# Hybrid decoder layer, one core: the last two blocks of the output projection multiplied together, and the up stage's tiles laid on the memory that comes free

## The chip, the cores and the metric

One core of a Trainium2 chip runs the whole layer in one program. The metric is the device time of one execution in microseconds (us), the median of several runs. Profiles are of one execution; times in rows count from the start of its span.

## What is computed

A decoder layer on x of 2048 tokens by 1024, all in float32. The first half mixes tokens with two groups of heads (attention and an mLSTM), whose outputs stand side by side in 1024 columns. The seam that matters here is what follows:

```python
mixed = jnp.concatenate([o_diff, o_mlstm], axis=-1) @ w_out   # 1024 x 1024
x = x + rmsnorm(mixed, norm_mix_post)
h = rmsnorm(x, norm_mlp_pre)
u = jnp.square(jax.nn.relu(h @ w_up))                         # 1024 x 4096
x = x + rmsnorm(u @ w_down, norm_mlp_post)
```

## The kernel before

**Matmuls.** TensorE multiplies float32r. Each operand is kept as a high part (a cast) and a low part (the rest), and each product is three matmuls of 128x128 by 128x512 (`mm3`, lines 91 to 95, and `product`, line 964).

**Output projection** (`out_proj`, line 838). The 2048 tokens are 16 blocks of 128, taken in the order `seq`; the first eight belong to g = 0, the last eight to g = 1. For each block, `gather` (line 853) loads the head outputs `od` into a `raw` tile, transposes them in two halves on TensorE into a PSUM tile `tp` of the two-buffer pool `psT`, and writes the operand into a tile `p`, of which there are two (pools `shp` and `ot`). `project` (line 858) runs over the eight weight rows `w[kc]` (128 rows of w_out each, 8 KB a partition, all in the pool `wo`) and both halves of the columns into two PSUM banks `po`: 48 matmuls. `residual` (line 869) loads the block's x into `xt` (one buffer), squares `po` on ACT, scales by an rsqrt on VectorE (DVE), adds x on POOL into `x1` (one buffer), stores x1, and makes the normed `t` for the MLP.

**Operands of the up stage.** The up and the down product use seven sub-products in place of eight, so the up stage wants seven combinations B1 to B7 of the normed tokens for each g. `spread` (line 908) transposes `t` of a block in two halves into `tp`, forms the combinations with DVE and POOL, and `parts` (line 895) casts each one on ACT and subtracts on DVE. For g = 0, B1, B2, B6 and B7 (`NEAR`) go straight into the tiles `ops` on the right side of the memory. All others go through a tile `hl` (two buffers) and a store into `Bd` in DRAM, 512 KB in runs of 512 B. A block of even place in a pair stores two parts for g = 1, one of odd place five (the last two through POOL). The spread of block n - 2 and the gather of block n + 1 stand between the weight rows of block n.

**Up stage** (`MlpUp`, line 973; `UpPair`, line 1020). For g = 0 and 1 there are 8 batches of two pairs; each batch takes the steps 1, 2, 6, 7, 5, 3, 4 (`UP_ORDER`), and a step is 12 matmuls for each pair. Its left operand comes from a row of w_up (`wr`, 256 KB), combined on DVE, cast on ACT (line 1059) and subtracted on DVE (line 1026) into a tile `w`. Steps 1, 6, 5 and 3 add into a bank A, copied by ACT between steps (`snap`); steps 2 and 7 begin a bank B, step 4 adds to the second. Tiles of one name are taken in turn from a ring of places (`Rotation`, line 820). B5, B3 and B4 of g = 0 are loaded (`load_op`, 2 MB each) into the pool `far`.

**What sets the order.** The framework lists the instructions of each engine and of SP's queue in the order in which its own timing model finds them ready, the program's order breaking ties; on the chip each engine works its list strictly in order. All loads and stores here are issued from SP's queue. A tile that lies on the memory of a closed pool waits for the readers of the tiles that it covers.

**The seam.** In `body` the pools `raw`, `wo` and `shp` lie at the left, `ops` at the right. Step 1 of the first two pairs (`first`, line 985) has two `wr` tiles, two `w` tiles and two PSUM banks of its own at the right (`wre`, `wqe`, `psE`). All else of the up stage is opened in `run` (line 994), behind the projection's pools: at the left first `far` and `sp`, then 15 tiles `u`, 12 `wr` and 4 `w`.

Of the kernel before, what the change touches and what calls it, by code (L numbers as in the profile page):

```python
# [20 lines left out]
S = 2048  # L21
# [77 lines left out]
def body(ctx: ExitStack, tc: tile.TileContext, a: dict, out: bass.AP, phases="ABCD"):  # L99
# [39 lines left out]
    with ExitStack() as mid:  # L139
        mix = phase_mix(tc, a, sc, ident, late)  # L140
        next(mix)
        for _ in first:
            pass
        raw = mid.enter_context(tc.tile_pool(name="raw", bufs=2, reuse_waits="tile"))
        wo = mid.enter_context(tc.tile_pool(name="wo", bufs=1, reuse_waits="tile"))
        w_out = [wo.tile([128, 2, D], F32R, name=f"wo{kc}") for kc in range(KC)]
        shp = mid.enter_context(tc.tile_pool(name="shp", bufs=1, reuse_waits="tile"))
        late.update(raw=raw, w_out=w_out, shp=shp)
        for _ in mix:
            pass  # L150
# [5 lines left out]
        early.append(hp.enter_context(  # L156
            tc.tile_pool(name="psE", bufs=1, side="right", reuse_waits="tile", space=PSUM)))
        up = out_proj(tc, a, sc, ident, ops, w_out, dn, raw, shp, late["oT"],
                      lambda: MlpUp(tc, a, sc, ops, hpool, *early))
    up.run()  # L160
    hp.close()
    mlp_down(tc, a, sc, out)
# [657 lines left out]
class Rotation:  # L820


    def __init__(self, shape, dt, name, *pools):
        self.shape, self.dt, self.name, self.places, self.n = shape, dt, name, [], 0
        for p, n in pools:
            self.extend(p, n)
# [8 lines left out]
        return pool.tile(self.shape, self.dt, name=name, bufs=1)  # L835


def out_proj(tc, a, sc, ident, ops, w, dn, raw, shp, oT, start_up):
    nc = tc.nc
    with ExitStack() as ctx:  # L840
        def pool(name, bufs, **kw):
            return ctx.enter_context(tc.tile_pool(name=name, bufs=bufs, reuse_waits="tile", **kw))

        ld = pool("ld", 2)
        ot = pool("ot", 1)
        cc = pool("cc", 1)
        t1 = pool("t1", 2)
        x1p = pool("x1p", 1)
        so = pool("so", 2)
        psO = pool("psO", 4, space=PSUM)  # L850
        psT = pool("psT2", 2, space=PSUM)
# [6 lines left out]
        def project(oT, between=()):  # L858
            po = [psO.tile([128, 512], F32, name="po") for _ in range(2)]
            for kc in range(KC):  # L860
                for hf in range(2):
                    sl = slice(hf * 512, hf * 512 + 512)
                    mm3(nc, po[hf], [oT[:, 0, kc, :], oT[:, 1, kc, :]], [w[kc][:, 0, sl], w[kc][:, 1, sl]],
                        kc == 0, kc == KC - 1)
                if kc % 2 == 0 and kc // 2 < len(between):
                    between[kc // 2]()
            return po

        def residual(tt, po):
            rows = slice(tt * 128, (tt + 1) * 128)  # L870
            xt = ld.tile([128, D], F32, name="xt", bufs=1)
# [68 lines left out]
        g2 = cc.tile([128, D], F32, name="g2")  # L940
        nc.sync.dma_start(g2, a["g_mlp_pre"].partition_broadcast(128))
        seq = [g * 8 + c + o * 4 for g in range(2) for c in range(4) for o in range(2)]
        h2 = {}
        for n, tt in enumerate(seq):
            between = []
            if n >= 2:
                half = spread(seq[n - 2], h2.pop(n - 2))
                between += [partial(half, 0), partial(half, 1)]
            cur = oT
            if n + 1 < NT:  # L950
                oT, half = gather(seq[n + 1], n + 1)
                between += [partial(half, 0), partial(half, 1)]
            po = project(cur, between)
            h2[n] = residual(tt, po)
        up = start_up()
        for n in (NT - 2, NT - 1):
            up.first(n - NT + 2)
            half = spread(seq[n], h2.pop(n))
            half(0)
            half(1)  # L960
        return up


def product(nc, ps, lhs, rhs, n, first, last):
# [8 lines left out]
class MlpUp:  # L973

    def __init__(self, tc, a, sc, ops, hpool, wre, wqe, psE):
        self.tc, self.nc, self.a, self.sc, self.ops, self.hpool = tc, tc.nc, a, sc, ops, hpool
        self.pools = wre, wqe, psE
        self.wr = Rotation([128, 512], F32, "wr", (wre, 2))  # L980
        self.wq = Rotation([128, 2, 512], F32R, "w", (wqe, 2))
        self.psA = Rotation([128, 512], F32, "A", (psE, 2))
        self.batch = [UpPair(self, 0, m) for m in range(2)]

    def first(self, m):

        self.batch[m].matmuls(1)

    def load_op(self, g, i):
        t = (self.hpool if i in NEAR else self.far).tile([128, 2, 4, 512], F32R, name=f"B{i}")  # L990
        self.nc.sync.dma_start(t.bitcast(F32), self.sc["Bd"][g, i])
        return t

    def run(self):
        wre, wqe, psE = self.pools
        with ExitStack() as ctx:
            def pool(name, bufs, **kw):
                return ctx.enter_context(self.tc.tile_pool(name=name, bufs=bufs, reuse_waits="tile", **kw))

            self.far = pool("far", 1)  # L1000
            self.sp = Rotation([128, 512], F32, "s", (pool("sp", 1), 5))
            self.up = Rotation([128, 512], F32, "u", (pool("up", 1), 15))
            self.wr.extend(pool("wr", 1), 12)
            self.wq.extend(pool("wq", 1), 4)
            self.psA.extend(pool("psA", 1, space=PSUM), 2)
            self.psB = Rotation([128, 512], F32, "B", (pool("psB", 1, space=PSUM), 4))
            for i in (5, 3, 4):
                self.ops[i] = self.load_op(0, i)
            for g in range(2):
                if g == 1:  # L1010
                    for i in UP_ORDER:
                        self.ops[i] = self.load_op(1, i)
                for n in range(8):
                    pairs = self.batch if (g, n) == (0, 0) else [UpPair(self, g, 2 * n + m) for m in range(2)]
                    for i in UP_ORDER:
                        for p in pairs:
                            p.run(i)


class UpPair:  # L1020
    def __init__(self, up, g, j):
        self.up, self.nc, self.g, self.j = up, up.nc, g, j
        self.begun = False

    def tt(self, out, x, y, op):
        self.nc.vector.tensor_tensor(out, x, y, op=op)  # L1026
# [24 lines left out]
        return {7: self.a21, 5: self.s1, 4: self.a22}[i]  # L1051

    def matmuls(self, i):
        if i == 1 and self.begun:
            return
        self.begun = True
        src = self.left(i)
        w = self.up.wq()
        self.nc.scalar.copy(w[:, 0], src)  # L1059
# [273 lines left out]
```

## Time and profile before

| | us |
|---|---|
| median of 3 runs | 2559.36 (2558.26 to 2561.15) |
| the profiled execution's own time | 2563.28 |
| its span, first to last instruction | 2561.4 |
| TensorE busy with matmuls | 2425.0 |
| DVE, ACT, POOL busy | 1456.0, 1065.2, 440.1 |

The span is cut into 40 slices of 64 us in the page's strips. PE stands for TensorE's matmuls; PEclk is the clock that it was granted, in tenths of full speed. In chains and timelines each line has its start in us, its length in us, and what ran; in square brackets stands the idle time before it and what ended that.

### The profile page before, as it was taken

To read this page: it belongs to the slowest core of one execution; us is meant where nothing else is said; L and a number is where in the kernel's file an instruction comes from. 1 tells how busy PE (TensorE), PEld (TensorE's weight loads), DVE (VectorE), ACT (ScalarE), POOL (GpSimd) and SP (SyncE) were. 2 spreads that over 40 slices of the span, in tenths; PEclk is the share of its full clock that TensorE was granted. 3 is DMA by queue.
4 is the path that set the end of the run, shared out by engine and by line. 5 is a ranking of instruction groups with operands and counts; after the bars stand their busy time and mean duration, and the time that the engine had idled before them with its cause. 6 is when DMAs were issued, how large, how long until landed. Compare 5 with 4: busy or idle time off the path is not lost.

```text
span 2561.4 us, 34625 instructions
## 1 busy us (share of the span) xinstructions
PE 2425.0 (95%) x12030; PEld 2040.0 (80%) x12030; DVE 1456.0 (57%) x3132; ACT 1065.2 (42%) x2103; POOL 440.1 (17%) x724
## 2 busy tenths in 40 slices
PE   8999999989879799999939999999999999999998
PEld 6888889987668687888828888888888888887886
DVE  4483441016657588576647667666665543333885
ACT  7210112326656577644524344444444332332433
POOL 0002222104635354432300000000000000000423
PEclk9999999998889899999969999999999999999999
DMA  9323432257653634255774345844358664444784
GB/s 320 130 78 91 125 109 85 55 133 167 145 115 75 148 88 113 83 177 181 236 266 164 136 157 174 350 161 168 133 176 305 222 221 169 146 143 167 282 288 144
DMA packets 296751, 424.35 MB, mean 166 GB/s; under 512 B 23584, under 2 KB 170416, under 8 KB 295040
## 3 DMA queue, kind: packets, MB, share of 16 engines
q1 hardware_dynamic: 296224, 421.94, 51.5%
q8 instruction: 95, 1.56, 0.3%
q14 instruction: 80, 0.66, 0.1%
q0 software_dynamic: 352, 0.20, 0.1%
HBM read 283.56 MB, written 138.49 MB: 165 GB/s over the span
## 4 chain that ended last, share of the span: by engine, by line
PE 76%; DMA 11%; DVE 6%; POOL 2%; ACT 2%; issue 2%; SPq 0%; POOLq 0%; DVEq 0%; ACTq 0%
PE pd L969 16%; PE A L969 14%; PE B L969 10%; PE pp L93 7%; PE pp L94 7%; PE pp L95 7%; DMA br<-in_w_down_dram 3%; PE pv L656 3%; PE s L573 3%; PE po L93 2%; DMA E<-Md 2%; PE po L94 2%; PE po L95 2%; PE tp L651 2%; DMA wb<-Wd 1%
## 5 line engine op out<-in xcount | busy, mean ns | idle before, releaser
L969 PE MATMUL pd<-bo,ao 128*128 128x512 f32 x2688 | 613.8, 390 | 8.3 <-DVE y L1153 4.8
L969 PEld LDWEIGHTS pd<-bo,ao 128*128 128x128 f32 x2688 | 506.2, 188 | 115.8 <-issue 5.2
L969 PE MATMUL A<-B,w 128*128 128x512 f32 x1536 | 359.3, 389 | 0.0
L969 PEld LDWEIGHTS A<-B,w 128*128 128x128 f32 x1536 | 288.3, 188 | 59.7
L969 PE MATMUL B<-B,w 128*128 128x512 f32 x1152 | 274.4, 392 | 19.2 <-ACT w L1059 19.2
L93 PE MATMUL pp<-w,xT 128*128 128x512 f32 (+1 forms) x768 | 271.3, 358 | 9.3 <-ACT w L230 7.8
L94 PE MATMUL pp<-w,xT 128*128 128x512 f32 (+1 forms) x768 | 273.2, 356 | 0.0
L95 PE MATMUL pp<-w,xT 128*128 128x512 f32 (+1 forms) x768 | 271.1, 355 | 0.0
L969 PEld LDWEIGHTS B<-B,w 128*128 128x128 f32 x1152 | 217.9, 189 | 65.0 <-ACT w L1059 19.7
L1211 POOL TENSOR_TENSOR y<-y,g 128x512 f32<-128x512 f32 x32 | 49.2, 1560 | 1183.6 <-ACT jk L1205 1120.2
L1178 ACT CAST ao<-ar 128x1024 fp32r<-128x1024 f32 x112 | 117.8, 1052 | 287.5 <-PE pd L969 150.5
L1153 DVE TENSOR_TENSOR ao<-ar,ao 128x1024 fp32r<-128x1024 f32 x112 | 139.3, 1243 | 152.3 <-ACT ao L1178 152.2
L1026 DVE TENSOR_TENSOR w<-wr,w 128x512 fp32r<-128x512 f32 x224 | 154.0, 689 | 105.0 <-ACT w L1059 103.9
L573 PE MATMUL s<-K,Q 128*128 128x512 f32 (+3 forms) x640 | 193.9, 418 | 13.6 <-DVE p L577 6.6
L1059 ACT CAST w<-wr 128x512 fp32r<-128x512 f32 x224 | 138.8, 621 | 130.6 <-PE B L969 116.8
L656 PE MATMUL pv<-V,pT 128*128 128x128 f32 x1088 | 158.2, 290 | 31.5 <-ACT pT L653 22.9
L656 PEld LDWEIGHTS pv<-V,pT 128*128 128x128 f32 x1088 | 147.4, 202 | 44.0 <-ACT pT L653 26.2
L586 ACT ACTIVATE p<-p,nm 128x128 f32<-128x128 f32 (+15 forms) x128 | 153.5, 1200 | 33.2 <-DVE nm L585 22.1
L93 PEld LDWEIGHTS pp<-w,xT 128*128 128x128 f32 x768 | 144.4, 188 | 25.9 <-ACT w L230 8.7
L577 DVE TENSOR_SCALAR_CACHE_REDUCE p<-s 128x512 f32<-128x512 f32 x192 | 129.0, 684 | 51.6 <-PE s L573 28.4
L94 PEld LDWEIGHTS pp<-w,xT 128*128 128x128 f32 x768 | 144.5, 188 | 15.2 <-DVE w L231 0.3
L95 PEld LDWEIGHTS pp<-w,xT 128*128 128x128 f32 x768 | 144.3, 188 | 15.1
(249 smaller groups left out, 3566.0 us busy)
## 6 DMA issues: line engine op xcount, KB each, us to landing
ud<-u SPq DMA_DIRECT2D x224, 256.0 KB, 2.8
ar<-ud SPq DMA_DIRECT2D x112, 512.0 KB, 4.1
br<-in_w_down_dram SPq DMA_DIRECT2D x224, 256.0 KB, 4.0
wr<-in_w_up_dram SPq DMA_DIRECT2D x128, 256.0 KB, 3.6
Bd<-hl SPq DMA_DIRECT2D x40, 512.0 KB, 3.9
B<-Bd SPq DMA_DIRECT2D x10, 2048.0 KB, 13.8
Q<-Qd SPq DMA_DIRECT2D x128, 128.0 KB, 4.7
raw<-in_xT_dram SPq DMA_DIRECT2D x32, 256.0 KB, 5.0
```

The source lines that it names most:

```text
L93: nc.tensor.matmul(ps, lhs[0], rhs[0], start=first, stop=False)
L94: nc.tensor.matmul(ps, lhs[0], rhs[1], start=False, stop=False)
L95: nc.tensor.matmul(ps, lhs[1], rhs[0], start=False, stop=last)
L573: nc.tensor.matmul(ps[:, :w], Q[:, var, c, qo:qo + 128], Ks[h, j][:, c, 0:w], start=(var == 0), stop=(var == 1))
L577: nc.vector.tensor_scalar(dst, ps[:, :w], 0.0, None, op0=ALU.add, op1=ALU.max, accum_out=mx[:, c, j:j + 1])
L586: nc.scalar.activation(pc[:, :W], pc[:, :W], AF.Exp, bias=nm[:, c:c + 1], accum_out=Z[:, c:c + 1])
L656: nc.tensor.matmul(pv, pT[:, i * 128:(i + 1) * 128], Vs[h, j][:, i, :], start=(b == 0), stop=(b == nb - 1))
L969: nc.tensor.matmul(ps, l[i], r[j], start=(first and k == 0 and m == 0), stop=(last and k == n - 1 and m == 2), skip_group_check=True)
L1026: self.nc.vector.tensor_tensor(out, x, y, op=op)
L1059: self.nc.scalar.copy(w[:, 0], src)
L1153: nc.vector.tensor_tensor(out, x, y, op=op)
L1178: nc.scalar.copy(l[:, 0], u)
```

## The change

The last two blocks are no longer multiplied one after the other. Block 13 carries the gathers of both 14 and 15; `project` then takes a list of operands and goes through the weight rows once, so that each row is used for both blocks before the next. For this there are three tiles `p` (a new pool `otp`) and three pairs of banks for `po`, one of which is `psE`. The projection's other pools move to the right side. When the joint loop is written, the left pools are closed (`mid.close()`), and the up stage's tiles are opened at the left on the rows of `raw`, `wo`, `shp` and `otp` in this order: 10 `wr`, 4 `w`, 5 `s`, `far`, 3 `u`. Its banks B and A follow on those of `po`, and at the end 12 `u`, 4 `wr`, 1 `w` and two banks B at the right on the projection's pools and on `psT`. So there are 14 `wr` as before, 5 `w` in place of 6, 15 `u`. Steps 1, 2 and 6 of the first batch and the loads of B5 and B3 are written between the residuals and the spreads of blocks 14 and 15; the load of B4 behind them. `first` and `begun` go.

```diff
-        early = [hp.enter_context(tc.tile_pool(name=n, bufs=1, side="right", reuse_waits="tile"))
-                 for n in ("wre", "wqe")]
...
+        up = MlpUp(tc, a, sc, ops, hpool, psE)
+        out_proj(tc, a, sc, ident, ops, w_out, dn, raw, shp, late["oT"], mid, up)
     up.run()
...
-            oT = (shp if n % 2 == 0 else ot).tile([128, S], F32, name="p")
+            oT = otp.tile([128, S], F32, name=f"p{n % 3}") if n % 3 else shp.tile([128, S], F32, name="p")
...
+        def project(n, oTs, between):
+
+            po = [[(psE if (n + i) % 3 == 1 else psO).tile(
+                [128, 512], F32, name=f"A{hf}" if (n + i) % 3 == 1 else f"po{(n + i) % 3}{hf}", bufs=1)
+                for hf in range(2)] for i in range(len(oTs))]
             for kc in range(KC):
...
+                for i, oT in enumerate(oTs):
+                    for hf in range(2):
+                        sl = slice(hf * 512, hf * 512 + 512)
+                        mm3(nc, po[i][hf], [oT[:, 0, kc, :], oT[:, 1, kc, :]], [w[kc][:, 0, sl], w[kc][:, 1, sl]],
+                            kc == 0, kc == KC - 1)
+                for half in between.pop(kc, ()):
+                    half()
             return po
...
+        nxt = [oT]
+        for n in range(NT - 2):
+            cur = nxt
+            nxt = []
+            between = {}
             if n >= 2:
...
+                between[0], between[2] = ([f] for f in halves(n - 2))
+            for i, m in enumerate([n + 1] if n < NT - 3 else [NT - 2, NT - 1]):
+                t, half = gather(seq[m], m)
+                nxt.append(t)
+                between[4 + 2 * i] = [partial(half, 0)] if n < NT - 3 else [partial(half, 0), partial(half, 1)]
+                if n < NT - 3:
+                    between[6] = [partial(half, 1)]
+            h2[n] = residual(seq[n], project(n, cur, between)[0])
+        last = NT - 2, NT - 1
+        between = {}
+        for n in last:
+            a0, a1 = halves(n - 2)
+            between[4 * (n - NT + 2)], between[4 * (n - NT + 2) + 2] = [a0], [a1]
+        po = project(NT - 2, nxt, between)
+        mid.close()
+        up.open_left()
+        up.step(0, 0, 1)
+        for n, q in zip(last, po):
+            h2[n] = residual(seq[n], q)
+        ps2.close()
+        up.open_psum()
+        up.step(0, 0, 2)
+        up.load_far(5)
+        for n, i in zip(last, (6, 7)):
+            for half in halves(n):
+                half()
+            if i == 6:
+                up.step(0, 0, 6)
+                up.load_far(3)
+    up.open_right()
+    up.load_far(4)
...
+    def open_left(self):
+        self.wr.extend(self.pool("wr"), 10)
+        self.wq.extend(self.pool("wq"), 4)
+        self.sp.extend(self.pool("sp"), 5)
+        self.far = self.pool("far")
+        self.up.extend(self.pool("up"), 3)
+
+    def open_psum(self):
+        self.psB.extend(self.pool("psB", space=PSUM), 2)
+        self.psA.extend(self.pool("psA", space=PSUM), 2)
+
+    def open_right(self):
+        self.up.extend(self.pool("upr", side="right"), 12)
+        self.wr.extend(self.pool("wrr", side="right"), 4)
+        self.wq.extend(self.pool("wqr", side="right"), 1)
+        self.psB.extend(self.pool("psB2", side="right", space=PSUM), 2)
...
+                for i in UP_ORDER[3 if (g, n) == (0, 0) else 0:]:
+                    self.step(g, n, i)
```

## Rows read from the trace of the kernel before

**Rows 1.** The page: TensorE's busy tenths and granted clock in 40 slices.
```profile
PE   8999999989879799999939999999999999999998
PEclk9999999998889899999969999999999999999999
```

**Rows 2.** Stretches: us, busy PE, PEld, DVE, ACT, POOL (instructions), granted clock, DMA share, GB/s.
```profile
1258.00:1280.00 22.00, 22.00 (x110) 18.22 (x109) 15.02 (x37) 9.99 (x22) 7.67 (x4) 1.00 0.74 221
1260.00:1263.00 3.00, 3.00 (x18) 2.52 (x17) 2.16 (x4) 1.68 (x3) 1.36 (x1) 1.00 0.99 263
1280.00:1324.00 44.00, 3.83 (x19) 2.40 (x17) 13.70 (x26) 10.30 (x22) 5.27 (x3) 0.56 0.91 301
1286.00:1296.00 10.00, 0.00 (x0) 0.00 (x0) 3.65 (x8) 1.90 (x4) 2.34 (x1) 0.50 1.01 431
1324.00:1328.00 4.00, 3.35 (x8) 2.64 (x9) 2.77 (x4) 1.70 (x3) 0.00 (x0) 0.50 0.96 315
1330.00:1332.00 2.00, 2.00 (x11) 1.62 (x10) 2.00 (x4) 1.42 (x3) 0.00 (x0) 1.00 0.29 94
```

**Rows 3.** Timeline of PE: last projection matmul, first of the up stage behind it.
```profile
1280.14 0.39 PE L95 MATMUL po<-wo,p 128*128 128x512 f32 x1
...
1324.65 0.80 PE L969 MATMUL B<-B,w 128*128 128x512 f32 x1 [19.16 <-ACT w L1059]
```

**Rows 4.** The chain of waits through the hole: start, length, what.
```profile
1283.67 17.81 DMA Bd<-hl
...
1302.84 3.53 DMA Bd<-hl
...
1316.83 0.63 ACT hl L901
...
1318.80 5.15 DMA wr<-in_w_up_dram
...
1324.65 9.52 PE B L969 x30
```

**Rows 5.** Waits from 1270 to 1340: us in total, times, longest.
```profile
ACT hl L901 <- DMA Bd<-hl: 22.2, 7, 10.2
...
PE B L969 <- ACT w L1059: 19.2, 1, 19.2
```

**Rows 6.** Timeline of SP's queue: issues of the operand and w_up loads.
```profile
1279.61 3.17 SPq L991 DMA_DIRECT2D B<-Bd  x3
1283.67 11.54 SPq L904 DMA_DIRECT2D Bd<-hl  x2
...
1318.80 11.90 SPq L1030 DMA_DIRECT2D wr<-in_w_up_dram  x11
```

**Rows 7.** The chain elsewhere: step 1 done early, eight transposes, a full step.
```profile
1186.74 4.78 PE A L969 x21
...
1241.55 0.87 PE tp L807 x8
...
1370.89 5.44 PE A L969 x24
```

**Rows 8.** Timelines of DVE, POOL and ACT: the residual of block 15.
```profile
1285.94 1.41 DVE L885 SCALAR_TENSOR_TENSOR t<-po,rr,g 128x512 f32<-128x512 f32 x2
...
1287.48 2.34 POOL L886 TENSOR_TENSOR x<-t,xt 128x1024 f32<-128x1024 f32 x1 [9.06 <-DVE t L885]
...
1289.85 1.06 ACT L889 ACTIVATE t<-x 128x1024 f32<-128x1024 f32 x1 [3.40 <-POOL x L886]
...
1292.38 1.28 DVE L892 SCALAR_TENSOR_TENSOR t<-x,r,g 128x1024 f32<-128x1024 f32 x1
```

**Rows 9.** The tile xt: 16 loads of 512 KB, from issue to landing.
```profile
DMA to landing us min/median/max: 3.2/4.5/6.8
```

**Rows 10.** Waits from 1400 to 1560, the steady up stage.
```profile
ACT w L1059 <- PE B L969: 32.4, 21, 2.1
DVE w L1026 <- ACT w L1059: 23.4, 22, 1.9
```

**Rows 11.** The page's groups: the casts of w.
```profile
L1059 ACT CAST w<-wr 128x512 fp32r<-128x512 f32 x224 | 138.8, 621 | 130.6 <-PE B L969 116.8
```

More of the change, by code (lines that the diff above doesn't have):

```diff
@@ L153, in body @@
         ops = {i: hpool.tile([128, 2, 4, 512], F32R, name=f"B{i}") for i in NEAR[::-1]}
-        early = [hp.enter_context(tc.tile_pool(name=n, bufs=1, side="right", reuse_waits="tile"))
-                 for n in ("wre", "wqe")]
[L156 to L159, printed above, removed]
+        psE = hp.enter_context(tc.tile_pool(name="psE", bufs=1, side="right", reuse_waits="tile", space=PSUM))
+        up = MlpUp(tc, a, sc, ops, hpool, psE)
+        out_proj(tc, a, sc, ident, ops, w_out, dn, raw, shp, late["oT"], mid, up)
     up.run()
@@ L835, in __call__, with out_proj, pool @@
         return pool.tile(self.shape, self.dt, name=name, bufs=1)
-def out_proj(tc, a, sc, ident, ops, w, dn, raw, shp, oT, start_up):
+def out_proj(tc, a, sc, ident, ops, w, dn, raw, shp, oT, mid, up):
     nc = tc.nc
     with ExitStack() as ctx:
[L841 to L851, printed above, removed]
+        def pool(name, bufs, to=ctx, **kw):
+            return to.enter_context(tc.tile_pool(name=name, bufs=bufs, reuse_waits="tile", **kw))
+        cc = pool("cc", 1, side="right")
+        ld = pool("ld", 1, side="right")
+        ot = pool("ot", 1, side="right")
+        t1 = pool("t1", 2, side="right")
+        x1p = pool("x1p", 1, side="right")
+        so = pool("so", 2, side="right")
+        otp = pool("otp", 1, to=mid)
+        ps2 = ExitStack()
+        psO = pool("psO", 1, to=ps2, space=PSUM)
+        psT = pool("psT2", 2, side="right", space=PSUM)
@@ L942, in out_proj, with halves @@
         seq = [g * 8 + c + o * 4 for g in range(2) for c in range(4) for o in range(2)]
+        psE = up.psE
         h2 = {}
-        for n, tt in enumerate(seq):
-            between = []
-            if n >= 2:
[L947 to L961, printed above, removed]
+        def halves(n):
+            half = spread(seq[n], h2.pop(n))
+            return [partial(half, b) for b in range(2)]
+        nxt = [oT]
[3 more added lines that the diff above has]
+            between = {}
+            if n >= 2:
+                between[0], between[2] = ([f] for f in halves(n - 2))
[29 more added lines that the diff above has]
+    up.load_far(4)
 def product(nc, ps, lhs, rhs, n, first, last):
@@ L973, with __init__, pool @@
 class MlpUp:
[L977 to L981, printed above, removed]
-        self.psA = Rotation([128, 512], F32, "A", (psE, 2))
-        self.batch = [UpPair(self, 0, m) for m in range(2)]
-    def first(self, m):
-        self.batch[m].matmuls(1)
+    def __init__(self, tc, a, sc, ops, hpool, psE):
+        self.tc, self.nc, self.a, self.sc, self.ops, self.hpool, self.psE = tc, tc.nc, a, sc, ops, hpool, psE
+        self.ctx = ExitStack()
+        self.wr = Rotation([128, 512], F32, "wr")
+        self.wq = Rotation([128, 2, 512], F32R, "w")
+        self.sp = Rotation([128, 512], F32, "s")
+        self.up = Rotation([128, 512], F32, "u")
+        self.psA = Rotation([128, 512], F32, "A", (psE, 2))
+        self.psB = Rotation([128, 512], F32, "B")
+        self.pairs = {}
+    def pool(self, name, **kw):
+        return self.ctx.enter_context(self.tc.tile_pool(name=name, bufs=1, reuse_waits="tile", **kw))
+    def open_left(self):
[12 more added lines that the diff above has]
+        self.psB.extend(self.pool("psB2", side="right", space=PSUM), 2)
     def load_op(self, g, i):
@@ L991, in load_op, with load_far, step @@
         self.nc.sync.dma_start(t.bitcast(F32), self.sc["Bd"][g, i])
-        return t
-    def run(self):
[L995 to L1017, printed above, removed]
+        self.ops[i] = t
+    def load_far(self, i):
+        self.load_op(0, i)
+    def step(self, g, n, i):
+        if i == 1:
+            self.pairs = [UpPair(self, g, 2 * n + m) for m in range(2)]
+        for p in self.pairs:
+            p.run(i)
+    def run(self):
+        for g in range(2):
+            if g == 1:
+                for i in UP_ORDER:
+                    self.load_op(1, i)
+            for n in range(8):
+                for i in UP_ORDER[3 if (g, n) == (0, 0) else 0:]:
+                    self.step(g, n, i)
+        self.ctx.close()
 class UpPair:
```

14 lines of the change are left out of this document (1 added, 13 removed).

## The prediction

> **What bounds the kernel now.** I read the page's slices first. Of the 40 one stands out: the one from 1280 to 1344 us has 3 tenths of TensorE (PE) and 0.6 of its clock, among neighbours of 9 and 9 [rows 1]. The table by stretches puts edges on it: until 1280 PE is full at a granted clock of 1.00, from 1280 to 1324 it works 3.83 of 44 us, from 1330 on it is full again [rows 2]. That is the seam that the change touches. The timeline of PE gives the ends: the last matmul of the output projection ends at 1280.14 + 0.39 = 1280.53, the first one of the up stage after it starts at 1324.65 [rows 3]; between them stand the 16 transposes of blocks 14 and 15. **The hole is 44.1 us.**
>
> Why it is open is read from the chain of waits: a store of an operand slice takes 17.81 us to land, then come three more of 3.5 us one behind the other with a cast and a subtraction between (the first stands there), the last one's issue, a w_up load of 5.15 us, a cast, and then PE [rows 4]. The table of waits says the same: ACT waits 22.2 us for `Bd` stores, PE 19.2 us for the cast of `w` [rows 5]. The queue's timeline shows two causes. The three operand loads of 2 MB (B5, B3, B4) are issued at 1279.61, ahead of the stores of blocks 13 to 15. And the w_up rows come last of all, at 1318.80, because their buffers lie where the `hl` tiles lay [rows 6].
>
> None of it is needed by the data: blocks 14 and 15 belong to g = 1, and the first 38 us of the up stage are g = 0, whose operands stand in `ops` or in DRAM. The hole is made by buffers and queues.
>
> **The change, part by part.** The sum is made against the profiled execution, 2563.28 us; that is 3.92 over the median of 2559.36, so 3.92 is taken off at the end. T0 is the end of the joint multiplication.
>
> *What can be won.* The hole is 44.1. Behind it PE starts slowly: 30 matmuls take 9.52 us where the steady stage does 24 in 5.44 [rows 4, 7], so 30 would take 6.80, and 2.72 are lost to the clock (0.50, the 1.2 GHz level, from 1324 to 1328; 1.00, or 2.4 GHz, from 1330 to 1332) [rows 2]. The 16 transposes stay; at 0.87 us for eight [rows 7] they are 1.7. Bound: 44.1 + 2.7 - 1.7 = **45.1 us**. Step 1, which is now done early, in the middle of the projection (24 matmuls near 1186, of which one row has 21) [rows 7], moves behind T0: T0 comes 5.44 earlier and 5.44 are added behind it, net nothing.
>
> *Two blocks together.* The same 96 matmuls in another order: no cost. Block 13 now carries the transposes of two gathers, four halves, each read by ACT and by VectorE (DVE), under its last four weight rows, half of a block's matmuls; today two halves are done there without a stop of PE. I take 0; if that cover fails, the joint loop starts up to 2 us late. The third p tile and the third pair of PSUM banks only loosen waits; 0.
>
> *w_up loads early.* Ten loads of 256 KB move from behind the hole to before T0. The last 22 us before the hole move 221 GB/s, 4.9 MB, at a busy share of 0.74; with 2.6 MB more it is 341 GB/s, above the 263 that a stretch of mostly `Bd` stores shows at a share of 0.99 [rows 2]. So stores land up to 3 us later. I take 0 for PE, since no transpose waits there now, and keep 3.
>
> *What PE has behind T0.* Steps 1, 2 and 6 need B1, B2, B6, which stand: 16.3 us, with block 14's transposes 17.2. Half of step 5 (2.7) may fit in; its other w tile lies on the tile `t` of block 15. Step 7 needs two more banks for B, and these lie on the two banks of the transposes: **the new wait.** It ends when block 15's halves have been read. Step 2's banks lie on block 15's own po: ACT's squares, the rsqrt and DVE's two reads took 6.8 us there (1280.53 to 1287.35) [rows 8], against 5.44 of step 1. I take 1.3; step 6 going first would make it 0.
>
> *When block 15 is read.* The x tile has one buffer, so block 15's x is loaded only behind block 14's add, which ends 9.3 us after the last matmul today (1289.82) [rows 8]; block 14's banks finish 1.4 earlier, so T0 + 8. An x load lands in 4.5 at the median [rows 9]: T0 + 12.5 at best. Then add 2.34, square and rsqrt 2.53 (1289.85 to 1292.38), scaling 1.28, and for half the transposes and the first subtraction 1.2, an estimate from eight in 0.87 [rows 7, 8]: 7.3. The first bank is free at T0 + 19.8 at best. But the loads of B5, B3, B4 become possible at about T0 as well, and today's schedule sends them as soon as their rows are free, ahead of stores that the program has first [rows 6]. A store behind them took 17.81 instead of 3.5 [rows 4]. If x stands behind them it lands near T0 + 18, and the banks come free at T0 + 25.3 and about 28.5 (two casts more). A check in bytes: 6.3 MB of loads, two x transfers and four stores, 9.4 MB, at the 300 GB/s that the hole runs at [rows 2] take 31 us. I take 25.3, since that is what this schedule has done with the same three loads.
>
> *A page against this step.* The Trainium skill ("DMA: Bandwidth & Descriptors", Specifications) gives 512 B as the least run for full rate, and 435 GB/s as that rate; the `Bd` runs are 512 B, so by it the 9.4 MB would take 21.6 us and the time would be about 2519. The trace does not agree: 263 GB/s at a share of 0.99 among stores, 431 only among the 2 MB loads [rows 2].
>
> *The sum.* PE is out of work at T0 + 17.2 to 19.9 and waits until 25.3: 5.4 to 8.1, I take 7. Between the halves of step 7, 28.5 - 25.3 - 2.7 = 0.5. Such a hole would end at the low clock: from 1286, 6 us after the last projection matmul, it is 0.50 [rows 2]; I put the 2.7 of today's restart. With the 1.3 before step 2: 11.5. Step 5, 3 and 4 have their operands by then. The second batch's rows lie on `ot` and `t`, free by T0 + 36 if today's last cast (1316.83) is no later [rows 4], and are wanted at T0 + 51: hidden. 45.1 - 11.5 = 33.6 us; 2563.28 - 33.6 - 3.92 = **2525.8**, or 2526. With stalls of 6 to 17 in all, 2520 to 2531.
>
> **The rivals.**
> *No wait (2517).* The operand loads are written one by one between the steps, 2 MB each. If the schedule keeps that, block 15 is read by T0 + 19.8 to 22.5, PE never stops for more than 2 us, the clock stays up: stalls of 0 to 5, 2514 to 2519. For it: the program's order. Against it: a like order was not kept today [rows 6].
>
> *Casts behind `hl` (2538).* ACT works in order. If the casts of step 6 or 7 are queued behind the `hl` casts of blocks 14 and 15, they wait as today until the last but one store, 1316.83 or T0 + 36 [rows 4]: from T0 + 17 on PE stands for 19 us, and 2.7 for the clock and 1.3 make 23: 2538, up to 2546 with the early loads' 3 and some of the 2 at the joint loop. For it: 22.2 us of exactly that wait [rows 5]; against it: steps 2 and 6 need no store, so their casts are ready before T0 + 7.
>
> *The rows are not freed (2559).* If the w_up loads are still issued behind the stores on SP's queue, the hole stays, with step 1 inside it, as long as today: 2559, within 0.2% (5 us, which is also about what a measurement of this kernel can tell from no change).
>
> *A ring of five (slower).* The w tiles go from 6 to 5 for the whole up stage, 224 of them. Today ACT's cast of a tile waits for PE to give a slot back (32.4 us in a stretch of 160, nearly all its waiting for casts) [rows 10], so PE is five products ahead, 13.6 us; with five slots four, 10.9. A cast, DVE's longest wait for one and a subtraction put at the cast's length are 0.62 + 1.9 + 0.62 = 3.1 [rows 10, 11]. Were they late all the same, the change would lose its gain from 33.6 / 224 = 0.15 us a tile on; at 0.3 the time is 2525.8 + 67 = 2593. Against it stand the 7.8 us between 3.1 and 10.9.
>
> **How the numbers follow.** Forecast 0.56 (2520 to 2531); no wait 0.21; casts behind `hl` 0.13; rows not freed 0.04; ring of five 0.06. The range takes in the first three, 0.90, with a little off at either end: 2514 to 2546. Faster by over 0.2%: 0.56 + 0.21 + 0.13 = 0.90; within 0.2%: 0.04; slower: 0.06.
>
> **What would show it.** In the changed kernel's trace: matmuls of A straight behind the last `po` one, wr loads issued before it, one hole of 5 to 10 us about 17 us later with step 7's B behind it, ended by `ta` or an `hl` subtraction that reads the transposes' bank; `Bd` or x transfers of over 10 us at that place; the low clock in that hole alone. Wrong would be: PE idle right behind T0 (the rows are not free), no hole at all, holes further on in the up stage with a cast as releaser (the ring), or PE below 20 of 20 us in the blocks before 1258.

## The result, and the profile after

The changed kernel takes 2539.75 us (2536.98 to 2544.12, 4 runs), the kernel before beside it 2559.39 (2558.26 to 2561.15, 4 runs): ratio 0.9924, interval 0.9907 to 0.9941. That is 19.6 us less. The forecast was 2526, with 2514 to 2546 as its range.

The profiled execution took 2536.98 us. The strips of the page, after:

```profile
PE   8999999998888799999989999999999999999998
PEclk9999999998989999999999999999999999999999
```

The slice with the 3 and a clock of 6 [rows 1] has an 8 and a 9 now; it runs from 1267.6 to 1330.9 here, since the span is shorter. The large hole is closed. What took its place is seen by stretches of 20 us, with two short ones inside (us, PE, PEld, DVE, ACT, POOL busy, granted clock, DMA share, GB/s). The last matmul of the joint loop ends at T0 = 1274.8.

```profile
1104.79:1274.79 170.00, 167.32 (x828) 137.46 (x828) 113.30 (x257) 79.46 (x181) 49.03 (x26) 1.00 0.64 200
1274.79:1294.79 20.00, 14.20 (x57) 10.76 (x56) 16.45 (x35) 9.61 (x22) 3.40 (x2) 0.91 0.97 342
1280.00:1282.00 2.00, 2.00 (x6) 1.52 (x6) 2.00 (x2) 0.13 (x1) 1.19 (x1) 0.50 1.18 386
1294.79:1314.79 20.00, 16.13 (x58) 12.05 (x58) 13.35 (x25) 8.05 (x16) 2.77 (x2) 0.83 1.04 395
1298.00:1302.00 4.00, 4.00 (x10) 3.13 (x11) 3.35 (x6) 0.00 (x0) 0.82 (x1) 0.50 1.13 420
1314.79:1334.79 20.00, 17.03 (x71) 13.18 (x72) 11.94 (x17) 7.04 (x13) 2.92 (x2) 1.00 0.80 239
1334.79:1354.79 20.00, 18.40 (x80) 14.48 (x80) 16.91 (x28) 8.70 (x16) 0.00 (x0) 1.00 0.68 244
1400.00:1700.00 300.00, 300.00 (x1325) 248.51 (x1324) 202.13 (x317) 124.65 (x223) 0.00 (x0) 1.00 0.55 203
```

PE lacks 14.2 us in the 80 us behind T0; from 1400 to 1700 it is full. The timeline of PE has the 14.2 us in twelve pieces:

```profile
1274.43 0.39 PE L95 MATMUL po<-wo,p 128*128 128x512 f32 x1
1276.97 0.73 PE L999 MATMUL A<-B,w 128*128 128x512 f32 x2 [2.16 <-ACT w L1099]
1279.01 6.93 PE L999 MATMUL A<-B,w 128*128 128x512 f32 x22 [1.30 <-DVE w L1069]
1287.79 1.06 PE L920 MATMUL tp<-ident,t 128*128 128x128 f32 x8 [1.85 <-DVE t L897]
1288.61 5.70 PE L999 MATMUL B<-B,w 128*128 128x512 f32 x24
1294.85 0.73 PE L999 MATMUL A<-B,w 128*128 128x512 f32 x2 [0.54 <-ACT w L1099]
1297.84 10.77 PE L999 MATMUL A<-B,w 128*128 128x512 f32 x34 [2.26 <-ACT w L1099]
1309.29 3.02 PE L999 MATMUL A<-B,w 128*128 128x512 f32 x12 [0.68 <-ACT s L1116]
1312.15 1.03 PE L920 MATMUL tp<-ident,t 128*128 128x128 f32 x8
1313.89 0.73 PE L999 MATMUL A<-B,w 128*128 128x512 f32 x2 [0.71 <-ACT w L1099]
1314.92 2.58 PE L999 MATMUL A<-B,w 128*128 128x512 f32 x10 [0.30 <-DVE w L1069]
1317.35 5.60 PE L999 MATMUL B<-B,w 128*128 128x512 f32 x24
1324.12 0.73 PE L999 MATMUL A<-B,w 128*128 128x512 f32 x2 [1.17 <-ACT w L1099]
1325.53 2.56 PE L999 MATMUL A<-B,w 128*128 128x512 f32 x10 [0.67 <-DVE w L1069]
...
1334.52 1.25 PE L999 MATMUL A<-B,w 128*128 128x512 f32 x4 [0.99 <-ACT w L1099]
```

The twelfth piece, 1.6 us, ends at T0 + 63.6 (a hole is named by its end here and below). Read the order of work: step 1, block 14's transposes, step 2, step 6 with step 5 (2, 34 and 12 matmuls), block 15's transposes, the first pair of step 3, and only then, at 1317.35, step 7, without a wait. The low clock shows in the lengths: the 24 of step 1 take 0.73 + 6.93 us, where 24 take 5.60 later.

The queue's timeline shows one reason why steps 1 and 6 are late:

```profile
1260.24 10.81 SPq L909 DMA_DIRECT2D Bd<-hl  x3
1271.14 0.62 SPq L1073 DMA_DIRECT2D wr<-in_w_up_dram  x1
1274.72 0.51 SPq L909 DMA_DIRECT2D Bd<-hl  x1
1275.28 0.66 SPq L1073 DMA_DIRECT2D wr<-in_w_up_dram  x1
...
1279.34 0.42 SPq L1040 DMA_DIRECT2D B<-Bd  x1
1279.80 2.40 SPq L1073 DMA_DIRECT2D wr<-in_w_up_dram  x4
```

Only one row of w_up is issued before T0, the second after it, and step 6's four rows behind the first 2 MB operand load. The last of them is in the chain of waits that leads to the hole of 2.26 us. It lands at 1292.15, and until the cast at 1297.17 DVE works through 5 us of its list, where the sums of rows for step 6 stand among parts of u and an `hl` subtraction:

```profile
1281.54 10.61 DMA wr<-in_w_up_dram
...
1293.54 0.67 DVE wr L1069 x2
...
1297.17 0.63 ACT w L1099
1297.84 10.78 PE A L999 x34
```

In step 1 the rows are not all of it. The first one had landed at 1275.09, 0.3 us behind T0. ACT cast it only at 1276.28, behind the squares of both blocks' `po`; DVE then made the low part behind block 14's residual, and that ended the stop of 1.30:

```profile
1276.28 0.64 ACT L1099 CAST w<-wr 128x512 fp32r<-128x512 f32 x1
1276.95 1.41 DVE L890 SCALAR_TENSOR_TENSOR t<-po,rr,g 128x512 f32<-128x512 f32 x2
1278.27 0.68 DVE L1069 TENSOR_TENSOR w<-wr,w 128x512 fp32r<-128x512 f32 x1
```

The waits from 1270 to 1340, beside [rows 5]:

```profile
POOL x L891 <- DMA xt<-in_x_dram: 20.0, 1, 20.0
...
ACT hl L906 <- DMA Bd<-hl: 13.3, 6, 4.2
...
PE A L999 <- ACT w L1099: 7.8, 6, 2.3
```

ACT still waits 13.3 us for `Bd` stores, and POOL waits 20 us for block 15's x.

**Where the gain went.** The start of the projection moves by some us from one execution to the next (1069.8 to 1079.1 in the profiles of this study), so the seam is read from there. The projection took 206.99 us before, step 1 included, and 204.99 after; the rest, from T0 to the end of the span, 1280.91 and 1260.31. Together 1487.9 and 1465.3: **22.6 us less** of the 45.1 that could be won. Of the 22.5 lost, 3.4 lie in the projection (204.99 - (206.99 - 5.44)), 14.2 are PE's holes, and 4.9 remain. The clock makes about that: it is at its lower level, 0.50 or 1.2 GHz, from 1280 to 1283.4 and from 1297 to 1303.8, together 10.2 us. PE works in 9.4 of them, and half of that, 4.7, is lost (an estimate). Both stretches begin behind two stops close together (2.16 and 1.30; 0.54 and 2.26). Behind the other eight stops the clock stays at 1.00.

### The profile page after: what moved, and what is told of

It is laid out like the page before. It is cut to its first block, busy times and chain, and to the rows that moved or that the text cites. A ratio compares the mean times of both kernels' runs of the same rounds, so it can differ in the third digit from the quotient of the medians.

```text
span 2535.1 us, 34590 instructions
## 1 busy us (share of the span) xinstructions
PE 2424.9 (96%) x12030; PEld 2035.6 (80%) x12030; DVE 1451.3 (57%) x3132; ACT 1057.8 (42%) x2103; POOL 439.5 (17%) x724
## 3 DMA queue, kind: packets, MB, share of 16 engines
q8 instruction: 95, 1.56, 0.3%
## 4 chain that ended last, share of the span: by engine, by line
PE 73%; DMA 12%; DVE 7%; POOL 3%; ACT 2%; issue 2%; SPq 1%; POOLq 0%; ACTq 0%; DVEq 0%
PE pd L999 16%; PE A L999 13%; PE B L999 10%; PE pp L93 7%; PE pp L95 7%; PE pp L94 7%; DMA br<-in_w_down_dram 3%; DMA E<-Md 2%; PE pv L653 2%; PE s L570 2%; DMA Q<-Qd 1%; PE po L93 1%; PE po L95 1%; PE po L94 1%; PE tp L648 1%
## 5 line engine op out<-in xcount | busy, mean ns | idle before, releaser
L999 PE MATMUL A<-B,w 128*128 128x512 f32 x1536 | 365.7, 393 | 12.4 <-ACT w L1099 7.8
L999 PEld LDWEIGHTS B<-B,w 128*128 128x128 f32 x1152 | 216.0, 188 | 45.1 <-ACT w L1099 0.4
```

The source lines that it names most:

```text
L999: nc.tensor.matmul(ps, l[i], r[j], start=(first and k == 0 and m == 0), stop=(last and k == n - 1 and m == 2), skip_group_check=True)
```

## The experiments

The theories: one late thing holds the seam (the rows of w_up, block 15's x, the operand loads ahead of the stores, the stores' short runs, the two `hl` tiles, the two blocks' spreads), against "lists": many inputs come late, every engine works its list in a fixed order, and taking one away only leads to the next. All ratios are to the kernel before, measured beside it (2559 us beside the changed kernel, 2564 to 2566 beside the experiments, so medians of different rows are compared by their ratios). The table gathers them; the rest is T0 to the span's end and the holes are PE's in the 100 us behind T0, both from the profile.

| run | median us | ratio, interval | projection | rest | holes |
|---|---|---|---|---|---|
| changed kernel | 2539.75 | 0.9924 (0.9907 to 0.9941) | 204.99 | 1260.31 | 14.2 |
| e1_serial | 2543.16 | 0.9908 (0.9889 to 0.9927) | 205.69 | 1258.91 | 11.5 |
| e2_late | 2547.15 | 0.9926 (0.9908 to 0.9943) | 204.99 | 1263.51 | 15.8 |
| e3_own | 2542.05 | 0.9907 (0.9889 to 0.9925) | 204.89 | 1259.31 | 13.9 |
| e4_behind | 2546.42 | 0.9925 (0.9907 to 0.9943) | 204.99 | 1263.31 | 15.3 |
| f0_after (changed kernel again) | 2543.71 | 0.9915 (0.9901 to 0.9928) | 204.99 | 1259.31 | 14.3 |
| f1_noload | 2554.03 | 0.9954 (0.9942 to 0.9967) | 204.99 | 1269.01 | 19.7 |
| f2_runs | 2540.69 | 0.9900 (0.9887 to 0.9914) | 204.99 | 1259.71 | 13.0 |
| f4_runs_serial | 2539.95 | 0.9903 (0.9888 to 0.9918) | 206.19 | 1258.81 | 12.7 |
| g1_nospread | 2541.23 | 0.9905 (0.9892 to 0.9918) | 204.89 | 1259.91 | 13.5 |
| g2_hl3 | 2547.62 | 0.9927 (0.9912 to 0.9941) | 205.49 | 1259.91 | 13.1 |
| g3_xt2 | 2545.53 | 0.9921 (0.9909 to 0.9934) | 204.99 | 1263.61 | 14.5 |
| f5_runs_all | 2536.86 | 0.9890 (0.9874 to 0.9907) | 205.59 | 1255.71 | 10.9 |

By the ratios only f1_noload stands apart from the changed kernel; the intervals of all others overlap with at least one of its two. What follows rests on single profiles, and the two of the changed kernel differ by 1.0 us in the rest and 0.1 in the holes.

**e1_serial: the joint loop undone, the tiles kept.** Blocks 14 and 15 one after the other, on the freed rows as in the change.

```diff
-        for n in range(NT - 2):
+        for n in range(NT - 1):
...
-        po = project(NT - 2, nxt, between)
+        po = project(NT - 1, nxt, {0: [a0], 2: [a1]})
```

> Blocks 14 and 15 are multiplied one after the other again, all else as changed. Theory T (what is left of the hole comes from transfers that stand in the wrong order on SP's queue: the first w_up rows are issued only when the left pools close, and block 15's x stands behind operand loads): x of 15 now goes ahead of the loads, the first rows do not, so some 5 us faster than the changed kernel, about 2535. Rival J (the two residuals and spreads that fall together behind the joint loop are what costs, on ACT and DVE): most of the 19 us left goes, 2525 or less. Rival R (freeing the weight rows one by one is what lets the tiles be loaded early): slower, 2545 to 2550.

Block 15's t was made at T0 + 13.1, where the changed kernel has it at T0 + 36. The last `hl` came at T0 + 50.3 all the same, where it has 52, and the rest is 1258.91. Neither rival J (2525 or less) nor rival R (2545 to 2550) came; theory T's 5 us are within the interval and not shown. So the joint multiplication is not what brings the gain, and the blocks may as well go one by one. What is left of the change is the tiles and banks on freed places; that these bring it follows by elimination.

**e2_late: operand loads later.** B5 is loaded behind step 6, B3 and B4 only when block 15's x1 exists.

```diff
-        up.load_far(5)
...
                 up.step(0, 0, 6)
-                up.load_far(3)
-    up.open_right()
-    up.load_far(4)
+                up.load_far(5)
+                up.load_far(3, held["x1"])
+                up.load_far(4, held["x1"])
+    up.open_right()
```

> The joint loop stays; the load of B5 is written behind step 6, and B3 and B4 wait for block 15's sum x1 through a tiny POOL write into their tiles. Theory T: step 6's rows and block 15's x no longer stand behind 6 MB, the hole in step 6 (2.8 us and some 3 of low clock) goes and the later ones shrink: 2530 to 2535. Rival J: no change, 2540 within 3.

The add of block 15 came 5 us sooner (T0 + 21.3), but the holes are 15.8: one of 5.42 us at T0 + 58 that waits for DVE's u is new. No gain. Step 6's stop, which theory T wanted to end, stayed too: its four rows landed 5 us sooner (the last at T0 + 11.9 in place of 17.3), yet PE waited 3.29 + 1.14 us for its casts in place of 0.54 + 2.26, and the casts waited 1.99 and 1.31 us for DVE's sums of rows. Late rows are not all of that stop.

**e3_own: step 1's rows on tiles of their own**, free from the start.

```diff
-        self.wr = Rotation([128, 512], F32, "wr")
+        self.wr = Rotation([128, 512], F32, "wr", (wre, 2))
```

> Step 1's two w_up rows get two tiles of their own (4 KB at the right, the left ring has 8 in place of 10), so they can be loaded long before the left pools close. Theory T: the first stops behind the joint loop (2.2 and 1.3 us, and some 2 of low clock) shrink, 2534 to 2537, if the operand loads that move ahead of block 15's x do not take it back. Rival J: no change, 2540 within 3.

The timeline of PE in this run, three of its waits:

```profile
1285.20 5.80 PE L1000 MATMUL A<-B,w 128*128 128x512 f32 x24 [1.56 <-ACT w L1100]
1295.78 1.94 PE L921 MATMUL tp<-ident,t 128*128 128x128 f32 x8 [4.78 <-DVE t L898]
...
1321.49 1.18 PE L921 MATMUL tp<-ident,t 128*128 128x128 f32 x8 [4.46 <-DVE t L898]
```

Step 1 runs in one piece and at full clock (1.00), 5.80 us where the changed kernel took 7.66 with a stop of 1.30 in it. The stop of 1.56 before it is left, with the rows there in time: the cast stands behind ACT's squares. What it gains is lost again at the transposes, which stand in PE's list before the next step and wait for t: 13.9 of holes in place of 14.2. Most of what follows is of this kind.

**e4_behind: the written order.** Steps 1, 2, 6 and the loads are written behind the spreads.

```diff
-        up.step(0, 0, 1)
...
+    up.open_right()
+    for i in (1, 2, 6):
+        up.step(0, 0, i)
+    for i in (5, 3, 4):
+        up.load_far(i)
```

> Steps 1, 2 and 6 and the loads of B5, B3 and B4 are written behind the spreads of blocks 14 and 15, after the right pools are opened; memory and joint loop as changed. If the order is set by when the framework's model finds an instruction ready, and the place in the program only breaks ties: same as the changed kernel, 2540 within 3. If the written place sets it: the three steps run behind the spreads, 16 us are lost, 2553 to 2559.

The three steps did not move behind the spreads: PE still does step 1 first and steps 2 and 6 ahead of block 15's transposes. The ratio is the changed kernel's; in the profile the holes are 15.3 and the rest 1263.31, 3 to 4 us more. The place in the program matters little here.

**f0_after, f1_noload.** The changed kernel again beside the next three, and a kernel that leaves out the loads of B5, B3 and B4 of g = 0 (those steps then multiply other operands).

```diff
-        up.load_far(5)
...
-                up.load_far(3)
...
-    up.load_far(4)
+    up.ops.update({5: up.ops[1], 3: up.ops[2], 4: up.ops[6]})
```

> The changed kernel again, on the chip of the three runs below: its ratio to the kernel before, 0.992 within 0.002, and from its profile the time from the last projection matmul to the end, 1260 within 4, as a measure of how far one profiled execution may be trusted.

> The loads of B5, B3 and B4 of g = 0 (6.3 MB) are left out; the up stage reads B1, B2 and B6 in their place for g = 0, so the output of the first 1024 tokens is another. Theory B (since the change the seam is bound by the bytes of its transfers: the DMA engines are 0.90 to 0.94 busy in the 60 us behind the projection in all five traces, whatever the order): 6.3 MB at 325 GB/s are 19 us, nearly all that is left: 15 to 19 faster than the changed kernel. Theory L (ACT's and DVE's lists hold PE up, casts behind stores of hl, whatever the bytes): 3 to 6 faster.

f0_after came as expected. f1_noload was slower than the changed kernel, by about 10 us (2554.03 against 2543.71). Three of PE's waits, a stretch from T0 + 20 on, then the queue, then ACT:

```profile
1286.22 0.74 PE L997 MATMUL A<-B,w 128*128 128x512 f32 x2 [2.15 <-ACT w L1097]
...
1298.59 0.78 PE L997 MATMUL A<-B,w 128*128 128x512 f32 x2 [3.45 <-ACT w L1097]
...
1346.52 3.78 PE L997 MATMUL B<-B,w 128*128 128x512 f32 x8 [9.81 <-DVE u L1067]
```

```profile
1304.09:1324.09 20.00, 20.00 (x94) 16.59 (x93) 14.03 (x24) 9.59 (x19) 5.81 (x3) 0.95 0.65 194
```

```profile
1327.40 1.70 SPq L1038 DMA_DIRECT2D B<-Bd  x2
1329.19 1.51 SPq L909 DMA_DIRECT2D Bd<-hl  x2
```

```profile
1343.09 0.62 ACT L906 CAST hl<-k 128x512 fp32r<-128x512 f32 x1 [12.62 <-DMA Bd<-hl]
```

With the loads of g = 0 gone, the list brought the loads of g = 1 forward, ahead of the last stores. A store behind them held ACT for 12.62 us, and PE for 9.81: the chain of the old hole [rows 4] in small. So this is no clean test of the traffic behind T0 as a whole. It does show two things. No operand load runs before 1327.40, T0 + 43. In the first 20 us of that the holes at T0 + 2.1 and 14.5 (2.15 and 3.45 us) are there all the same, so operand loads are not the cause of these. In the next 20 us PE is full, where the changed kernel has 16.13 (15.84 in f0_after), and the first pair of step 4 ends at T0 + 52.6 in place of some 56 (an estimate from the 24 that end at T0 + 58.7): up to there the run is some 3.3 us ahead, at the low end of theory L's 3 to 6, and then loses three times that in the hole of 9.81.

**f2_runs, f4_runs_serial: the operands in DRAM in runs of 4 KB** in place of 512 B; f4 also has e1's edit.

```diff
-        Bd={(g, i): dram(f"Bd{g}_{i}", (128, 2, 4, 512))
+        Bd={(g, i): dram(f"Bd{g}_{i}", (128, 4, 2, 4, 128))
```

> The operands B lie in DRAM and in SBUF as [128, 4 blocks, 2, 4, 128], so that a block's store has runs of 4 KB in place of 512 B; TensorE reads its 512 columns in four runs. Same bytes, same counts of transfers. Theory B: the stores near the seam take 1.2 us of the engines at 431 GB/s in place of 1.8 to 2 at 263 to 290, some 14 of them: 5 to 9 faster than the changed kernel. Theory L: within 3 of it. If the broken runs slow TensorE's reads, all of the up stage is longer and the time goes up.

> The long runs of f2_runs and the two blocks one after the other as in e1_serial. Theory B: as f2_runs, within 3, since the bytes are the same. If block 15's late x were what is left, faster than f2_runs by 5 or more.

The packets of the projection stage, from 1080 to 1260, fell from 32397 to 9464 for the same 33 MB, the median store from 4.3 to 4.1 us, ACT's waiting for stores behind T0 from 13.3 to 10.7 (the longest stayed at 4.3). The rest is 1259.71 and 1258.81. The ratios are lower than the changed kernel's, within their intervals. By the rest, theory B's 5 to 9 us did not come (the ratios are too wide to part them from none); nor did the broken runs slow TensorE. The shorter runs do cost the engines something: over these 180 us the queue's transfers take a share of 58.5% with runs of 512 B and 52.3% with runs of 4 KB. The rest did not get shorter by that.

**g1_nospread: the last two spreads left out.** Blocks 10 and 11 store their parts a second time in place of those of 14 and 15, inside the projection.

```diff
-            for half in halves(n):
-                half()
             if i == 6:
```

> Leaves out the spreads of the last two blocks (their transposes, parts, casts and stores); blocks 10 and 11 store their parts a second time in their place, inside the projection. This asks what the two spreads cost the first batch of the up stage altogether. Theory 'lists' (step casts, residuals and spreads share the in-order lists of ScalarE and VectorE, so that any one that is late holds the others): of TensorE's 14 us of holes behind the last matmul of the projection at most 6 stay (the first weight row and step 6's), 1.7 us of transposes go, the clock's loss of 5 falls to 2 or 3; the rest is 1246 to 1250 us where the changed kernel has 1259.3, and the ratio to the kernel before 0.9865 to 0.9885. Theory 'weight rows' (the holes belong to the late rows of w_up and of nothing else): only the transposes go, rest 1257 to 1258, ratio 0.990 to 0.9915.

Neither came. No transposes, no `hl` casts and no stores of the last two blocks stand in the way, and still the rest is 1259.91. Two of PE's waits in this run:

```profile
1283.77 8.91 PE L999 MATMUL A<-B,w 128*128 128x512 f32 x24 [5.84 <-ACT w L1099]
1295.72 7.33 PE L999 MATMUL B<-B,w 128*128 128x512 f32 x24 [3.04 <-DVE t L890]
```

Step 1 came later still (5.84 us of hole, where its two stops made 3.46 in the changed kernel), and the clock fell to 0.79 in these 20 us. From T0 - 10 to T0 + 50 the queue moved 18.5 MB, against 18.0 in the changed kernel: the list fills the place of the stores with later rows and stores of u. Nor is the test clean: the seven stores that blocks 10 and 11 make in addition fall into the projection, and the first row of w_up landed at T0 + 3.6 (T0 + 0.3 in the changed kernel) and was cast at T0 + 5.2, behind `hl` casts that waited for stores. So g1 doesn't clear the spreads; it shows that the seam stays as long without those of blocks 14 and 15.

**g2_hl3 and g3_xt2: a third `hl` tile, a second x tile** (both with two tiles u moved to the other side for the room).

```diff
-                hl = ot.tile([128, 2, 4, 128], F32R, name="hl", bufs=2)
+                hl = ot.tile([128, 2, 4, 128], F32R, name="hl", bufs=3)
```

```diff
-        ld = pool("ld", 1, side="right")
+        ld = pool("ld", 2, side="right")
```

> A third tile for the parts hl (two tiles of u are moved to the other side for its room). Theory 'stores' (ScalarE's casts stand behind an hl tile whose store has not landed, 13 us of waiting in the changed kernel): that waiting falls under 5 us, the last hl store is issued 5 us or more earlier than 51 us behind the projection's end, holes fall from 14 to 8 to 10, rest 1253 to 1255, ratio 0.988 to 0.990. Theory 'lists': the waiting moves to the next thing (x, DVE's list, the queue's order), rest 1257 to 1261, ratio 0.990 to 0.9925, as the changed kernel.

> A second tile for x's rows, so that block 15's are requested without waiting for block 14's addition (same two tiles of u moved). Theory 'x is late' (block 15's addition came 26 us behind the projection's end, where the kernel before had it at 7): the addition is at 8 to 10, block 15's t at 15 to 18, the last hl 10 us or more before 51, rest 1252 to 1255, ratio 0.988 to 0.990. Theory 'lists': block 15's t comes early, as with the blocks one after the other, and the last hl and the rest stay: last hl 48 to 52, rest 1257 to 1261, ratio 0.990 to 0.9925.

Waits of g2_hl3, then POOL's timeline of g3_xt2:

```profile
PE tp L920 <- DVE t L897: 7.1, 2, 4.4
ACT hl L906 <- DMA Bd<-hl: 6.8, 3, 3.2
```

```profile
1305.87 2.53 POOL L891 TENSOR_TENSOR x<-t,xt 128x1024 f32<-128x1024 f32 x1 [18.54 <-DMA x1d<-x]
```

With a third `hl`, ACT's wait for stores halved, to 6.8 us, short of the 5 that theory 'stores' set, and PE waited 7.1 us for t (1.85 in the changed kernel); the holes were 13.1. With a second x tile the add waits 18.54 us for the store of block 14's x1, because x1 has one tile too. So g3 did not bring block 15 forward, and its question was answered by e1 alone.

**f5_runs_all: three reliefs at once** (e1, e3 and f2).

> Three reliefs at once, each of which alone left the rest at 1259 to 1260 us: own tiles for step 1's rows, the last blocks one after the other, operands stored in runs of 4 KB. Theory 'one after another' (each relief lets the list come to its next late input, so that several together do add up): holes behind the projection fall from 14 to 5 to 9, rest 1250 to 1255, ratio 0.986 to 0.989. Theory 'one floor' (something shared sets the end of the first batch whatever comes early, such as the traffic of 300 to 350 GB/s in these 60 us): holes 12 to 15, rest 1257 to 1261, ratio 0.9895 to 0.9915.

The rest is 1255.71 and the holes are 10.9: between the two. The gain behind T0 is 3.6 us against f0_after. It has the lowest ratio of all, 0.9890; its interval (0.9874 to 0.9907) still overlaps that of the changed kernel (0.9901 to 0.9928), so the gain is seen in one profile and not shown by the times.

**What is settled and what is open.** The single reliefs that reached what they aimed at (step 1's rows in e3, block 15's x in e1, the operand loads in e2 and f1, the runs in f2) left the rest at 1258.9 or more, against 1260.3 and 1259.3 in the changed kernel; in e2, e3 and f1 the trace shows what was won being lost at a later stop with another releaser. That no one of them holds the seam alone is shown so far. Not tried: tiles of their own for step 6's rows. The second x tile did not reach its aim, the third `hl` only in part, and f1 and g1 changed more than they were to. That three together give back a few us fits "lists", which is argued and not shown. What the last 10.9 us of holes would need is open. So is how much the traffic as such does: the transfers fill a share of 0.97 and 1.04 of the first two 20 us in the changed kernel and of 0.87 to 1.06 in the variants; only f1 thinned it out, to 0.80 and 0.65, and it was ahead until its loads came.

## Why the prediction was right, and where it was not

**What held PE up was read rightly.** The hole of buffers and queues closed, step 1 stands behind T0, and the seam came out 22.6 us shorter of the 45.1 that were put as the most. The losses were put at 11.5 and were 22.5. The time fell into the range, 9 us above the forecast's own 2520 to 2531, because one large term was absent and several that stood at 0 were not 0: the number was saved by the width of the range, not by the sum. The one hole of 5 to 10 us that was to show it did not come. Two of the signs of being wrong came, in small: PE idle right behind T0 (2.16 us) and below full in the projection (167.32 of 170 us).

**The step that failed is "the new wait".** Step 7 was to stand 7 + 0.5 us on the transposes' banks from T0 + 17.2 on. The half of it that was a date held: block 15's x came late behind the loads, its add began at T0 + 26.4, its transposes were done at T0 + 38.4, and the last reads of the two banks at T0 + 39 and 44.5, later than the 25.3 and 28.5 that I took. But PE did not wait for it: the list puts 5 and the first pair of 3 ahead of 7, which then starts at T0 + 42.5 without a wait. I had counted half of step 5 as cover and kept the program's order for the rest, though [rows 6] had shown that the list does not keep it.

**"w_up loads early" was mis-sized.** Ten loads were to be issued before T0; one was, and the term stood at 0 with 3 kept. Step 1's two stops take 2.16 + 1.30 = 3.5 us, step 6's 0.54 + 2.26 = 2.8, not all of it by the rows. The new tiles lie on pools that close with the joint loop, and their loads stand at the end of SP's list of that stage, among stores; that the one comes of the other is argued from e3, where two tiles that are free from the start had their rows in time. e3 gives the rows' part of step 1 as well: with early rows the stop is 1.56, so 1.9 of the 3.5 were the rows', and step 1 is at full clock. The rest is ACT's and DVE's lists, in which casts and subtractions of w stand behind the two blocks' residuals; for that the sum had no term.

**"Two blocks together" was mis-sized too:** 0 with up to 2 kept, 3.4 measured. It is not the joint loop. PE waits 0.48 us for a gather's cast ahead of four blocks, every second one up to T0 - 64, and 1.2 us in three stops from 1104 to 1108, 3.1 in all; the kernel before has 0.1 us of stops in its projection:

```profile
1132.75 0.50 PE L93 MATMUL po<-wo,p 128*128 128x512 f32 x1 [0.48 <-ACT p L808]
```

There ACT squares the banks of the block just done (1130.74 to 1132.02) ahead of the gather's cast; in the kernel before the cast came first (1133.53 there, the squares at 1134.58). e1_serial, without the joint loop, has it as well (205.69). I argued that a third p tile and a third pair of banks only loosen waits; which of the two changes the order was not tried.

**The wait before step 2** was 1.3 in the forecast and 1.85 in the trace, but at the transposes of block 14 instead of at the banks. The banks were late as well: DVE read block 15's `po` until T0 + 14.2, where the sum had 6.8, but step 2 began only at T0 + 13.8, behind those transposes. **The clock** was 2.7 for one restart; 4.9 were lost, in two restarts, each behind two stops close together, where I had expected one behind a long hole.

**The rivals.** "Casts behind `hl`" gives 2538, close to the median, but that is luck: PE does not stand 19 us from T0 + 17. (By its own terms it is 2563.28 - 3.92 - 45.1 + 23 = 2537, and with 3 and 2 more 2542, so the 2546 does not follow from them.) A small form of the mechanism is there. ACT waits 13.3 us for stores, and casts of w stand behind some of them; the four holes from T0 + 49 on make 4.4 us. "No wait" was right on step 7 and wrong on the sum. "Rows not freed" fell: the rows are issued from 1271 on, not behind the last store. "A ring of five" fell: PE is busy 300.00 of 300 us from 1400 to 1700.

**The page on descriptors**, set against the trace in the forecast: with runs of 4 KB a store landed in 4.1 us instead of 4.3, and the rest did not change by more than repeats do. By this measure the short runs cost little, which is what the Trainium skill ("DMA: Bandwidth & Descriptors", Specifications) says of 512 B. By the engines' time they cost more: 33.1 MB at a share of 58.5% over 180 us are 314 GB/s at a full share, 33.2 MB at 52.3% are 353 (estimates). So the runs may account for a part of the gap between 263 and 431 GB/s that I held against the page [rows 2]; the rest of it no run here explains.

## What to carry to other kernels

Closing a hole that one chain of buffers and queues makes is worth its whole length only if all the inputs of the work behind it come in time. List for the first 50 us behind it when each input is issued, lands and is read, in the order of each engine's list and not of the program, and put a price on each that comes within a few us. Tiles laid on pools that close at the seam got their first loads there, among the last stores; two small tiles of their own for the first step's rows took its stops from 3.5 to 1.6 us here, though the seam as a whole did not get shorter by more than repeats differ. Where several lists are tight at once, judge a single relief by the holes that come behind it, and try reliefs together.

## What was not expected of the hardware

A subtraction on DVE that reads two tiles of SBUF waited inside its own time for POOL's add. DVE's timeline of the changed kernel, then POOL's:

```profile
1279.46 2.28 DVE L907 TENSOR_TENSOR hl<-k,hl 128x512 fp32r<-128x512 f32 x1 [0.51 <-ACT hl L906]
...
1282.52 0.69 DVE L907 TENSOR_TENSOR hl<-k,hl 128x512 fp32r<-128x512 f32 x1 [0.18 <-ACT hl L906]
```

```profile
1278.49 2.70 POOL L891 TENSOR_TENSOR x<-t,xt 128x1024 f32<-128x1024 f32 x1 [3.01 <-issue]
```

The first one takes 2.28 us, the second, the same operation with POOL idle, 0.69. It ends 0.55 us behind the add; in f0_after the same one takes 2.29, in g2_hl3, where it starts before the add, 0.69. The Trainium skill ("SBUF — State Buffer", Who interferes with whom) has this as a lock: a DVE instruction with two inputs in SBUF and a POOL instruction that reads SBUF contend for a shared port, and the later one waits. The traces agree, with 1.6 us. No row names it as a wait: it looks like a long operation.

A row of w_up, 256 KB, lands in 3.9 to 11.2 us from 1270 to 1300, with a median of 9.2; the long ones are issued behind the 2 MB loads.
